# One hybrid decoder layer on one core: key low halves padded to 128 rows, sample and first prompt steps spaced otherwise, LayerNorm offset on another engine

## The chip, the cores and the metric

The kernel runs on one core of one Trainium2 chip. The core has a matrix engine (PE in the profile, with its weight loads shown apart as PEld), a vector engine (DVE), a scalar engine (ACT), a general engine (POOL, GpSimd) and an engine that here only issues transfers (SP, SyncE). Each engine works through its own list of instructions in a fixed order and waits on semaphores for the others. Sums of matrix products are collected in PSUM, a memory of eight banks; all else lies in SBUF or in the chip's main memory. The metric is the device time of one execution, in microseconds (us); smaller is better.

## What is computed

One layer for a prompt of 1024 positions and 8 samples of 4 new positions (32 rows), 1056 rows in all, model width 2048. The reference, cut to its core:

```python
z = rms_norm(x, norm_g) @ w_in                       # 2048 -> 7168
q, k, v, ga, u, vc, gb = split(z)                    # 7 x 1024
q, k = rope(q), rope(k)                              # 16 heads x 64
vc = layer_norm(gelu(vc), ln_g, ln_b); u = gelu(u)
o_attn = dilated_attention(q, k, v)                  # (128,1), (512,4), (2048,16), merged
o_chunk = u * (tril(w_s) @ vc + b_s)                 # chunks of 128 positions, 8 groups of 128
y = rms_norm(x + concat(o_attn * silu(ga), o_chunk * silu(gb)) @ w_out, final_g)
```

The samples attend to a cache of keys and values as well; of each sample 896 cached positions matter. Keys, values and the normalised `vc` are outputs too.

## The kernel before

**Products.** Every float32 operand of a product is split into a float16 high part and a float16 low part. A product is then three passes, high by high, high by low and low by high, summed in one PSUM bank. The projections (`proj_chunk`, line 181) take most of PE: 72 column tiles of 128 columns (56 of the input projection, 16 of the output projection), each 16 blocks of the contraction times 3 passes, over 1056 rows cut into 3 chunks of 352. One chunk is thus 48 matrix instructions of 128x352. There are three banks for the sums (`ps_p`), so a chunk can start only when the chunk three before it has been read.

**Fillers.** All other work is cut into steps, put in a queue by `set_steps` and called by `fill` after every 6 projection products. Each step has a cost that is only a place in the queue: steps are spread evenly by cost over the products of one or two column tiles. A step `wait(c)` does nothing and only takes up room. The instructions that a step issues are then ordered for each engine by a scheduler, so an engine can find the work of a later step ahead of that of an earlier one.

**Periods.** After eight column tiles for the gated channel input comes period 0, with the value, query and key tiles of the first head pair, and beside it the LayerNorm (`ln_steps`) of nine row tiles. For each: DVE adds the high and low part (L401), takes statistics (L414, L415), POOL takes a power (L245), DVE scales (L423, L424), POOL adds the offset `lb` (L428), ACT and DVE split the result again (L146, L147). In the same stretch DVE does the rotary step (`rope`, L468 to L475), which reads the two sums of query and key columns out of the banks, and the low parts of the weights (L139).

Then come eight periods, one for each head pair. A period has five or six column tiles. Beside the first ones run the prompt's attention (`prompt_steps`): 16 items, a query tile of 128 by a head, in slots that do the scores of one item (`fa`), the softmax of the one before (`fb`), the values of the one three before (`fc`) and the gate. A score is two instructions into one bank: L610 multiplies the query (high and low, 128 rows) by the key's high half (`khd`, the same 64 rows twice), and L611 multiplies the query's high 64 rows by the key's low half in `klo`, whose rows 0 to 63 belong to head 0 and rows 64 to 127 to head 1. The probabilities are turned by a transfer (L647) and multiplied by the values (L658, L665).

Beside the last two tiles of a period (`run_ab`, queries and keys of the next head pair) run the samples (`sample_steps`). For each of 8 samples `prep` splits the cached keys (hi on ACT L719, lo on DVE L722), loads two preparations further on (`load`, L711; two raw buffers `kvr`, three buffers each for `kvh` and `kvl`), and `s_mm` multiplies them (L750, L751). Then `soft1` turns the scores on PE (L770), takes minimum, exponential and quotient (L773, L785, L788), `soft2` turns the probabilities by a transfer (L798), and `pv_new` (L807) and `pv_mm` (L818, L819) multiply by the values, prepared in the same way with the hi part on POOL (L721).

The chunk mixing (`mix`) sums in a bank of `ps_t` (two banks, shared with the gate's and the samples' transposes), adds the bias into an SBUF tile `cf` (L901), multiplies by the gate (L902) and splits (L146, L147).

Of the kernel before, what the change touches and what calls it, by code (L numbers as in the profile page):

```python
# [8 lines left out]
F32 = mybir.dt.float32  # L9
# [45 lines left out]
def hybrid_step_kernel(  # L55
# [51 lines left out]

# [1 line left out]
    w_raw = {}  # L109
# [38 lines left out]

# [1 line left out]
    queue = []  # L150
# [37 lines left out]

# [1 line left out]
    def gelu2(ps, n, tp, *outs):  # L190
# [13 lines left out]

    # =============== start: normalised activations, first columns ===============
    tmp = pool("tmp")
# [141 lines left out]

    # =============== remaining columns of the gated channel input ===============
    SP.dma_start(out=lg, in_=ln_g.partition_broadcast(128))  # L350
# [18 lines left out]
    def spread(steps, at):  # L369
        # steps placed `at` steps apart  # L370
        out = []
        for c, f in steps:
            out += [(1e-3, lambda: None)] * at + [(c, f)]
        return out
# [17 lines left out]

    # =============== LayerNorm of the channel input ===============
    def ln_steps(i):
        t0, n = TILES[i]
        gt = {}

        def f0():
            if i < NQ:
                g = lnp.tile([128, 1024], F32, tag="gt", name="gt", bufs=3)  # L400
                DVE.tensor_tensor(out=g, in0=gnat[:, 0, i, :], in1=gnat[:, 1, i, :], op=ALU.add)  # L401
            else:
                vc_sample(0)
                vc_sample(4)
                g = gnat_s
            gt[0] = g

        def f1():
            f0()
            g = gt[0]  # L410
            bs = lnp.tile([128, 2, 6], F32, tag="bs", name="bs", bufs=2)
            mv = lnp.tile([128, 2], F32, tag="mv", name="mv", bufs=2)
            for hh in range(2):
                DVE.bn_stats(bs[0:n, hh, :], g[:, hh * 512:(hh + 1) * 512])  # L414
            DVE.bn_aggr(mv[0:n], bs[0:n])  # L415
            r = lnp.tile([128, 1], F32, tag="lr", name="lr", bufs=2)
            rsqrt(r[0:n], mv[0:n, 1:2], n, 1.0, lnp, "lm", EPS * VCS * VCS)
            st_[i] = (mv, r)

        def f2():  # L420
            mv, r = st_.pop(i)
            g = gt[0]
            DVE.tensor_scalar(g, g, mv[0:n, 0:1], r[0:n], ALU.subtract, ALU.mult)  # L423
            DVE.tensor_tensor(out=g, in0=g, in1=lg[0:n], op=ALU.mult)  # L424

        def f3():
            g = gt[0]
            POOL.tensor_tensor(out=g, in0=g, in1=lb[0:n], op=ALU.add)  # L428

        st_ = ln_state  # L430

        def f4():
            g = gt.pop(0)
            o = gnat[:, :, i, :] if i < NQ else lnp.tile([128, 2, 1024], F16, tag="gt", name="gt", bufs=3)
            hilo(g, o[0:n, 0, :], o[0:n, 1, :], VRS)
            SP.dma_start(out=vr_d[i, 0:n], in_=o[0:n])
            if i == NQ:
                SP.dma_start(out=vch, in_=g)

        return [(0.1, f1), (0.1, f2), (0.1, f3), (0.1, f4)]  # L440

    ln_state = {}

    # =============== per head pair / channel group ===============
    mid = pool("mid", left2)
# [7 lines left out]
    khd = [mid.tile([128, S], F16, name=f"khd{h}") for h in range(2)]  # L453
    klo = mid.tile([128, S], F16, name="klo")
    qbd = mid.tile([128, 2, DB, 2, DS], F16, name="qbd")
# [3 lines left out]
    gb = mid.tile([128, T], F32, name="gb")  # L459
    POOL.memset(qbd, 0.0)  # L460

    def rope(p, pa, pb, c0, n):
# [33 lines left out]
    def stack_load():  # L496
        for h in range(2):
            SP.dma_start(out=qst[h], in_=q_d[h].rearrange("l x r n -> (l x r) n"))
            kk = k_d[h].rearrange("l x r n -> l (x r) n")
            SP.dma_start(out=khd[h][0:64], in_=kk[0])  # L500
            SP.dma_start(out=khd[h][64:128], in_=kk[0])
            SP.dma_start(out=klo[64 * h:64 * h + 64], in_=kk[1])

# [33 lines left out]

    # period 0: first head pair, with the LayerNorm beside it
    MV, MA, MB, MG, MU, MGB = {}, {}, {}, {}, {}, {}
# [41 lines left out]

    # =============== attention and mixing pools ===============
    right = ExitStack()
# [9 lines left out]
    def prompt_steps(p):  # L593
        """per (query tile, head): scores, softmax, values; returns slots"""
        items = [(t, h) for t in range(NQ) for h in range(2)]
# [4 lines left out]
        def fa(i):  # L600
# [4 lines left out]
            tq = slice(t * 128, (t + 1) * 128)  # L605
            hi0 = 64 * h
            for j0 in range(0, nk, 512):
# [4 lines left out]
                    out=ps[:, 0:n],  # L612
                    lhsT=qst[h][hi0:hi0 + 64, tq],
                    rhs=klo[hi0:hi0 + 64, j0:j0 + n],
                    start=False,
# [70 lines left out]
        for s in range(n + 4):  # L686
            fs = []
            cost = 1.2
            if s - 4 >= 0 and (s - 4) % 2 == 1:
# [12 lines left out]
    def sample_steps(p, ahl):  # L702
# [139 lines left out]
        pre = [(0.05, lambda: load(0)), (0.05, lambda: load(1))]  # L842
        s1 = [(0.1, lambda: prep(0)), (0.2, s_new), (0.2, lambda: prep(1))]
        for b in range(DB):
            s1.append((0.4, lambda b=b: (s_mm(b), prep(b + 2))))
        s2 = [wait(0.8), (0.4, soft1), wait(1.0), (0.4, soft2), wait(0.6), (0.1, pv_new)]
        for b in range(DB):
# [30 lines left out]
    def mix(g, part, direct=False):  # L878
# [10 lines left out]
        else:  # L889
# [5 lines left out]
            bias = bb[:, 128:160]  # L895
        cf = ap_.tile([128, 512], F32, tag="cf", name="cf", bufs=1)
        if part < 2:
            o3, i3 = cf.rearrange("p (a b) -> p a b", a=4), pm.rearrange("p (a b) -> p a b", a=4)
        else:
            o3, i3 = cf[:, 0:n], pm[:, 0:n]  # L900
        DVE.scalar_tensor_tensor(out=o3, in0=i3, scalar=1.0 / (VRS * SWS), in1=bias, op0=ALU.mult, op1=ALU.add)  # L901
        DVE.tensor_tensor(out=cf[:, 0:n], in0=cf[:, 0:n], in1=gb[:, c0:c0 + n], op=ALU.mult)  # L902
# [105 lines left out]

    # =============== output projection ===============
    yt = {}  # L1010
# [76 lines left out]
    def sq(i, part):  # L1087
        """adds to the sum of squares, then scales by the final gain"""
        o, n = rows(i)
        c = slice(PARTS[part], PARTS[part + 1])  # L1090
        j = bank(ps_s, "s")
        ACT.activation(  # L1092
            out=j[0:n, 0:c.stop - c.start], in_=o[:, c], func=AF.Square, accum_out=ssq[0:n, i, part:part + 1]
        )
        DVE.tensor_tensor(out=o[:, c], in0=o[:, c], in1=fg[0:n, c], op=ALU.mult)  # L1095
# [21 lines left out]
    for j in range(1, NOUT - 2):  # L1117
# [9 lines left out]
        drain()  # L1127
    # the last two column tiles: rows are finished as their products end
    J = NOUT - 2
# [71 lines left out]
def _period(p):  # L1201
    """the column tiles of the input projection between two stages of the attention, in order"""
    if p == 0:
# [97 lines left out]
```

## Time and profile before

| | |
|---|---|
| time, median of 3 runs | 1927.72 us (1921.68 to 1928.16) |
| span of the profiled execution | 1919.8 us |
| busy: PE, DVE, ACT, POOL | 1839.0, 1081.7, 726.5, 142.4 us |
| projection products of 128x352 (three groups) | 9792 instructions |
| scores with the key's low half, L611 | 192 instructions, 64.1 us |

The span runs from the first to the last instruction of one profiled execution; the page prints no separate whole time for that execution, so what lies around the span is taken as the 7.9 us between it and the median. In the rows of a profile, `out<-in` names the tiles of the program, `xN` counts instructions, and a time in brackets is how long the engine stood idle before the instruction and what ended that. Matrix instructions overlap: their durations are longer than the distance from one start to the next, and it is this distance that counts.

### The profile page before, as it was taken

The page shows a single profiled execution, that of the slowest core. Times are in us where ns is not written, and L with a number is a line of the kernel's source. Part 1 is how long each engine was busy: PE and PEld are TensorE (multiplying, and loading weights), DVE is VectorE, ACT ScalarE, POOL GpSimd, SP SyncE. Part 2 cuts the span into 40 slices and gives each one's busy share as a digit, 9 for nine tenths or more (in the row PEclk, how much of TensorE's full clock was granted, in tenths as well). Part 3 has the DMA queues.
Part 4 walks back from the last instruction along what each step waited for, and adds up shares of the span by engine and source line. Part 5 has one row for each costly group of instructions (what it writes and reads, how often), then busy time and mean ns, then how long its engine had stood idle before and what let it go on. Part 6 is the DMA issues. An engine that isn't in the chain of part 4 may idle for free. (4 is left out here: it accounts for less than half of the span.)

```text
span 1919.8 us, 37195 instructions
## 1 busy us (share of the span) xinstructions
PE 1839.0 (96%) x15040; PEld 1222.4 (64%) x15040; DVE 1081.7 (56%) x2383; ACT 726.5 (38%) x1605; POOL 142.4 (7%) x146
## 2 busy tenths in 40 slices
PE   8999969999999999999999999999999999999997
PEld 7866645666566666666656666656666666666667
DVE  7633696646655665565556557557557543423344
ACT  7523214632542453254245236336336311212224
POOL 0000140001001000100100010010010020000001
PEclk9999989999999999999999999999999999999999
DMA  7423327566555646665565565566666598322324
GB/s 257 125 66 71 96 94 207 101 162 182 133 109 159 201 95 162 190 122 122 172 167 107 155 197 130 145 189 134 170 186 126 134 323 231 86 67 67 71 62 182
DMA packets 340415, 276.13 MB, mean 144 GB/s; under 512 B 255890, under 2 KB 291730, under 8 KB 338130
## 3 DMA queue, kind: packets, MB, share of 16 engines
q1 hardware_dynamic: 340242, 273.76, 54.8%
q8 instruction: 117, 1.92, 0.4%
q14 instruction: 56, 0.45, 0.1%
HBM read 179.85 MB, written 38.26 MB: 114 GB/s over the span
## 5 line engine op out<-in xcount | busy, mean ns | idle before, releaser
L181 PE MATMUL proj<-xh,wh 128*128 128x352 f16 (+3 forms) x3712 | 1113.7, 304 | 15.5 <-DVE ta L473 12.8
L181 PE MATMUL proj<-xh,wl 128*128 128x352 f16 (+3 forms) x3712 | 1112.1, 304 | 2.6 <-DVE wl L139 2.6
L181 PE MATMUL proj<-xl,wh 128*128 128x352 f16 (+3 forms) x3712 | 1112.3, 304 | 1.2 <-DVE xl L147 1.2
L181 PEld LDWEIGHTS <-wh 128*128 128x128 f16 x7424 | 692.0, 98 | 342.0 <-issue 27.1
L181 PEld LDWEIGHTS <-wl 128*128 128x128 f16 x3712 | 364.1, 98 | 176.9 <-DVE wl L139 3.2
L139 DVE SCALAR_TENSOR_TENSOR wl<-wraw,wh 128x512 f16<-128x512 f32 x288 | 198.1, 717 | 131.8 <-ACT wh L138 131.1
L138 ACT ACTIVATE wh<-wraw 128x512 f16<-128x512 f32 x288 | 166.0, 620 | 171.4 <-PE proj L181 163.8
L722 DVE SCALAR_TENSOR_TENSOR kvl<-kvr,kvh 128x896 f16<-128x896 f32 x128 | 141.7, 1107 | 133.7 <-ACT kvh L719 65.6
L631 ACT ACTIVATE sp<-sp,mn 128x256 f32<-128x256 f32 (+7 forms) x128 | 98.9, 772 | 133.1 <-DVE mn L619 133.1
L147 DVE SCALAR_TENSOR_TENSOR pn<-sp,pn 128x512 f16<-128x512 f32 (+2 forms) x192 | 106.1, 564 | 38.2 <-ACT pn L146 36.5
L721 POOL TENSOR_SCALAR kvh<-kvr 128x896 f16<-128x896 f32 x64 | 72.2, 1129 | 436.6 <-DMA kvr<-in_vc 197.1
L619 DVE CUSTOM_DVE_ANT_0 sp<-s,mp 128x512 f32<-128x512 f32 (+3 forms) x128 | 74.1, 584 | 50.9 <-PE s L611 49.7
L146 ACT ACTIVATE pn<-sp 128x512 f16<-128x512 f32 (+2 forms) x192 | 94.4, 515 | 7.5 <-DMA pt<-pn 4.9
L719 ACT ACTIVATE kvh<-kvr 128x896 f16<-128x896 f32 x64 | 60.6, 948 | 72.9 <-DMA kvr<-in_kc 60.4
L658 PE MATMUL o<-vst,pt 128*128 128x128 f16 x576 | 66.5, 220 | 9.0 <-DMA pt<-pn 9.0
L147 DVE SCALAR_TENSOR_TENSOR yhl<-proj,yhl 128x352 f16<-128x352 f32 (+1 forms) x42 | 21.4, 510 | 89.3 <-ACT yhl L146 89.3
L146 ACT ACTIVATE yhl<-proj 128x352 f16<-128x352 f32 (+1 forms) x42 | 18.8, 448 | 134.8 <-PE proj L181 115.4
L925 POOL TENSOR_TENSOR gb<-gb,tb 128x352 f32<-128x352 f32 x24 | 25.6, 1065 | 551.5 <-DVE tb L203 551.5
L638 DVE RECIPROCAL r<-den 128x1 f32<-128x1 f32 x128 | 20.8, 162 | 79.4 <-ACT sp L631 79.1
L611 PE MATMUL s<-klo,qst 64*128 64x512 f16 (+2 forms) x192 | 64.1, 334 | 0.3 <-DMA klo<-k_d 0.3
L610 PE MATMUL s<-khd,qst 128*128 128x512 f16 (+2 forms) x192 | 62.3, 331 | 1.5 <-DMA khd<-k_d 1.5
L665 PE MATMUL o<-vst,pt 128*128 128x64 f16 x576 | 62.9, 193 | 0.0
(166 smaller groups left out, 1569.5 us busy)
## 6 DMA issues: line engine op xcount, KB each, us to landing
wraw<-in_w_in SPq DMA_DIRECT2D x110, 512.0 KB, 5.0
kvr<-in_kc SPq DMA_DIRECT2D x64, 448.0 KB, 4.3
kvr<-in_vc SPq DMA_DIRECT2D x64, 448.0 KB, 3.8
wraw<-in_w_out SPq DMA_DIRECT2D x32, 512.0 KB, 5.1
yn<-in_x SPq DMA_DIRECT2D x8, 1024.0 KB, 8.7
out_y_p<-yn SPq DMA_DIRECT2D x16, 512.0 KB, 3.5
xn<-in_x SPq DMA_DIRECT2D x7, 1024.0 KB, 6.3
out_v_o<-tb SPq DMA_DIRECT2D x24, 176.0 KB, 2.5
```

Of the source, the lines that this page charges most:

```text
L138: ACT.activation(out=hi[:, sl, :], in_=r[:, rs, :], func=AF.Copy, scale=WS)
L139: DVE.scalar_tensor_tensor(out=lo[:, sl, :], in0=r[:, rs, :], scalar=WS, in1=hi[:, sl, :], op0=ALU.mult, op1=ALU.subtract)
L146: ACT.activation(out=hi, in_=src, func=AF.Copy, scale=scale)
L147: DVE.scalar_tensor_tensor(out=lo, in0=src, scalar=scale, in1=hi, op0=ALU.mult, op1=ALU.subtract)
L181: PE.matmul(out=ps[:, 0:n], lhsT=a[:, k, :], rhs=b[:, k, c0:c0 + n], start=(i == 0), stop=(i == 3 * KT - 1))
L611: PE.matmul(out=ps[:, 0:n], lhsT=qst[h][hi0:hi0 + 64, tq], rhs=klo[hi0:hi0 + 64, j0:j0 + n], start=False, stop=True,)
L619: DVE.tensor_tensor_reduce(sp[:, j0:j0 + n], ps[:, 0:n], mp[:, S - nk + j0:S - nk + j0 + n], 1.0 / (QS * KS), prev, ALU.add, ALU.min, mn,)
L631: ACT.activation(out=sp[:, 0:nk], in_=sp[:, 0:nk], func=AF.Exp, scale=-1.0, bias=prev, accum_out=den)
L658: PE.matmul(out=o[:, 0:128].rearrange("p (l c) -> p l c", l=2), lhsT=pt[:, j], rhs=vst[:, :, kb, h * HD:(h + 1) * HD], start=(kb == 0), st ...
L665: PE.matmul(out=o[:, 0:64], lhsT=pt[:, w + j], rhs=vst[:, 0, kb, h * HD:(h + 1) * HD], start=False, stop=(kb == nb - 1))
L721: POOL.tensor_scalar(hi, r, VS, 1.0, ALU.mult, ALU.mult)
L722: DVE.scalar_tensor_tensor(out=lo, in0=r, scalar=KS if j < DB else VS, in1=hi, op0=ALU.mult, op1=ALU.subtract)
```

## The change

Four things are changed.

1. The key's low half gets a tile for each head, `klo[0]` and `klo[1]`, of 128 rows, with the rows of the other head set to zero once. The second score instruction then takes all 128 rows of the query and of `klo[h]`.
2. The first five slots of a prompt block get the cost 2.0 instead of 1.2. In the samples' steps the second preparation comes ahead of `s_new`, a `wait(0.8)` stands ahead of the first `s_mm`, and the wait ahead of `pv_new` is 1.4 instead of 0.6.
3. The LayerNorm's offset is added by DVE instead of POOL.
4. The chunk mixing works in place in its PSUM bank; the tile `cf` is gone.

```diff
-            POOL.tensor_tensor(out=g, in0=g, in1=lb[0:n], op=ALU.add)
+            DVE.tensor_tensor(out=g, in0=g, in1=lb[0:n], op=ALU.add)
...
-    klo = mid.tile([128, S], F16, name="klo")
+    klo = [mid.tile([128, S], F16, name=f"klo{h}") for h in range(2)]
...
+    for h in range(2):
+        POOL.memset(klo[h][64 - 64 * h:128 - 64 * h], 0.0)
...
-            SP.dma_start(out=klo[64 * h:64 * h + 64], in_=kk[1])
+            SP.dma_start(out=klo[h][64 * h:64 * h + 64], in_=kk[1])
...
-            hi0 = 64 * h
...
-                    lhsT=qst[h][hi0:hi0 + 64, tq],
-                    rhs=klo[hi0:hi0 + 64, j0:j0 + n],
+                    lhsT=qst[h][:, tq],
+                    rhs=klo[h][:, j0:j0 + n],
...
-            cost = 1.2
+            cost = 1.2 if s > 4 else 2.0
...
-        s1 = [(0.1, lambda: prep(0)), (0.2, s_new), (0.2, lambda: prep(1))]
+        s1 = [(0.1, lambda: prep(0)), (0.1, lambda: prep(1)), (0.2, s_new), wait(0.8)]
...
-        s2 = [wait(0.8), (0.4, soft1), wait(1.0), (0.4, soft2), wait(0.6), (0.1, pv_new)]
+        s2 = [wait(0.8), (0.4, soft1), wait(1.0), (0.4, soft2), wait(1.4), (0.1, pv_new)]
...
-        cf = ap_.tile([128, 512], F32, tag="cf", name="cf", bufs=1)
-        if part < 2:
-            o3, i3 = cf.rearrange("p (a b) -> p a b", a=4), pm.rearrange("p (a b) -> p a b", a=4)
-        else:
-            o3, i3 = cf[:, 0:n], pm[:, 0:n]
-        DVE.scalar_tensor_tensor(out=o3, in0=i3, scalar=1.0 / (VRS * SWS), in1=bias, op0=ALU.mult, op1=ALU.add)
+        cf = pm
+        o3 = pm.rearrange("p (a b) -> p a b", a=4) if part < 2 else pm[:, 0:n]
+        DVE.scalar_tensor_tensor(out=o3, in0=o3, scalar=1.0 / (VRS * SWS), in1=bias, op0=ALU.mult, op1=ALU.add)
```

The lists of instructions show where this lands. First DVE in period 0, around the rotary step of the first chunk of 352 rows (`proj` are the sums of query and key columns, `gt` a LayerNorm tile, `gnat` its split result, `bs`, `mv` and `lm` its statistics). Before:

```order
L401 TENSOR_TENSOR gt<-gnat 128x1024
L415 BN_AGGR mv<-bs 128x2
L414 BN_STATS bs<-gt 128x6
L469 TENSOR_TENSOR tb<-proj,sin_t 128x352
L244 TENSOR_SCALAR lm<-mv 128x1
L147 SCALAR_TENSOR_TENSOR gnat<-gt,gnat 128x1024
L470 TENSOR_TENSOR o_3096<-ta,tb 128x352
L423 TENSOR_SCALAR gt<-gt,mv,lr 128x1024
L473 TENSOR_TENSOR ta<-proj,cos_t 128x352
L474 TENSOR_TENSOR tb<-proj,sin_t 128x352
```

And with the change (lines after the klo tiles are numbered two higher, so L471, L475 and L476 are the old L469, L473 and L474):

```order
L428 TENSOR_TENSOR gt<-gt,lb 128x1024
L244 TENSOR_SCALAR lm<-mv 128x1
L401 TENSOR_TENSOR gt<-gnat 128x1024
L423 TENSOR_SCALAR gt<-gt,mv,lr 128x1024
L414 BN_STATS bs<-gt 128x6
L424 TENSOR_TENSOR gt<-gt,lg 128x1024
L471 TENSOR_TENSOR tb<-proj,sin_t 128x352
L414 BN_STATS bs<-gt 128x6
L472 TENSOR_TENSOR o_3099<-ta,tb 128x352
L415 BN_AGGR mv<-bs 128x2
L147 SCALAR_TENSOR_TENSOR gnat<-gt,gnat 128x1024
L475 TENSOR_TENSOR ta<-proj,cos_t 128x352
```

The offset (L428) now stands on DVE; four of the nine come ahead of the last read of the first query sum (L474, now L476, the row behind the last one shown), and one L401, one L423, one L414 and one L147, which stood ahead of that read, stand behind it.

Second, DVE in the samples' softmax of the second period, from the ninth preparation on (`kvl` is a preparation's low part, `ss` the turned scores). Before:

```order
L722 SCALAR_TENSOR_TENSOR kvl<-kvr,kvh 128x896
L147 SCALAR_TENSOR_TENSOR qkhl<-o_7289,qkhl 128x704
L722 SCALAR_TENSOR_TENSOR kvl<-kvr,kvh 128x896
L773 ISA ss,mn<-t,msk 64x512
L773 ISA mn 64x1
L773 ISA ss,mn<-t,msk,mn 64x416
L773 ISA mn 64x1
L468 TENSOR_TENSOR ta<-proj,cos_t 128x352
L787 RECIPROCAL r<-den 64x1
```

And with the change:

```order
L723 SCALAR_TENSOR_TENSOR kvl<-kvr,kvh 128x896
L147 SCALAR_TENSOR_TENSOR qkhl<-o_7286,qkhl 128x704
L774 ISA ss,mn<-t,msk 64x512
L774 ISA mn 64x1
L723 SCALAR_TENSOR_TENSOR kvl<-kvr,kvh 128x896
L470 TENSOR_TENSOR ta<-proj,cos_t 128x352
L774 ISA ss,mn<-t,msk,mn 64x416
L774 ISA mn 64x1
L788 RECIPROCAL r<-den 64x1
```

The first half of the minimum moves ahead of the eleventh preparation's low part, and the second half moves behind the rotary step's first read (L470, the old L468). On PE, in the same period, 24 projection products instead of 18 stand between `s_new` and the first `s_mm`, 42 instead of 48 between the first and the sixth `s_mm`, 25 instead of 35 between the last `s_mm` and the turning of the scores (L770), and 72 instead of 60 between that and `pv_new`.

## The prediction

> **What bounds the kernel now.** I began with the page's busy times and the granted clock, then asked for PE's waits.
>
> ```profile
> span 1919.8 us, 37195 instructions
> PE 1839.0 (96%) x15040; PEld 1222.4 (64%) x15040; DVE 1081.7 (56%) x2383; ACT 726.5 (38%) x1605; POOL 142.4 (7%) x146
> core 0: 1919.8 us, clock 0.988
> ```
>
> PE is busy for 96% of the span, so PE sets the end and an edit pays only where it shortens PE's own work, one of its waits, or the time at a lower clock. The mean clock of 0.988 means that 0.012 x 1919.8 = 23 us were lost to a lower clock. The waits say where PE stood still:
>
> ```profile
> PE o L807 <- DMA pst<-pn: 12.9, 8, 2.3
> PE proj L181 <- DVE ta L473: 12.8, 2, 7.6
> PE s L750 <- ACT kvh L719: 10.0, 8, 2.7
> PE s L751 <- DVE kvl L722: 9.0, 11, 0.9
> PE o L658 <- DMA pt<-pn: 9.0, 10, 3.3
> ...
> PE proj L181 <- DVE wl L139: 2.6, 1, 2.6
> ...
> PE s L610 <- DMA khd<-k_d: 1.5, 3, 0.8
> ```
>
> The columns are total us, times and longest us. The samples cost 12.9 + 10.0 + 9.0 us, two places in the LayerNorm 12.8 + 2.6, the first prompt tiles 9.0 + 1.5. But a wait is not all that PE can lose, so I read the distances from start to start where the scores stand among other products:
>
> ```profile
> 498.53 0.19 PE L665 MATMUL o<-vst,pt 128*128 128x64 f16 x1
> ...
> 498.65 0.38 PE L610 MATMUL s<-khd,qst 128*128 128x512 f16 x1
> 498.96 0.39 PE L611 MATMUL s<-klo,qst 64*128 64x512 f16 x1
> 499.28 0.32 PE L181 MATMUL proj<-xh,wh 128*128 128x352 f16 x1
> 499.44 0.31 PE L181 MATMUL proj<-xl,wh 128*128 128x352 f16 x1
> 499.59 0.31 PE L181 MATMUL proj<-xh,wl 128*128 128x352 f16 x1
> ```
>
> A projection product of 352 columns takes 0.15 us from start to start. In proportion, 512 columns should take 0.15 x 512/352 = 0.218. L610 takes 0.31 until the 64-row L611 begins, and L611 takes 0.32 until the 128-row L181 begins: about 0.09 lost on entering the 64-row shape and 0.10 on leaving it. No wait names this loss.
>
> **The zero-padded low half.** There are 192 such instructions:
>
> ```profile
> L611 PE MATMUL s<-klo,qst 64*128 64x512 f16 (+2 forms) x192 | 64.1, 334 | 0.3 <-DMA klo<-k_d 0.3
> ```
>
> With 128 rows the second score has the shape of its neighbours. A product's length goes by its columns, which stay, so the padding itself costs nothing: L610 with 128 rows and L611 with 64 both show 0.38 to 0.39. The gain is 192 x (0.31 + 0.32 - 2 x 0.218) = 192 x 0.194 = **37 us**. Bounds: 0 if the gap belongs to the instruction and not to the shape, 37 if all of it goes. I take 37, since full-height neighbours such as L658 and L665 in the same list follow each other without a gap. The two memsets run once, at the opening of the pool, on an engine that is busy for 142 us in all and idle at that place; nothing on PE waits for them, and if something did, two instructions no longer than POOL's 2.34 us add (below) would cost 5 us once. The loads move the same bytes.
>
> The Trainium skill has a rule for this and one against it, on the page "TensorEngine Tiling (Array Packing)": under Key Properties, that a change of the tiling mode drains the engine, with which these rows agree at 0.09 to 0.10 us, and under Theoretical Speedup, that a contraction of at most 64 can go up to twice as fast in tiles of its own, which padding gives up. By the second this term would be no gain; it is weighed as a rival below.
>
> **The LayerNorm offset on DVE.** In the stretch from 214 to 300 us DVE is the bound:
>
> ```profile
> 214.00:300.00 86.00, 70.65 (x450) 45.01 (x448) 81.45 (x107) 21.28 (x32) 31.18 (x18) 0.94 0.39 116
> 256.03 2.34 POOL L428 TENSOR_TENSOR gt<-gt,lb 128x1024 f32<-128x1024 f32 x1 [2.72 <-DVE gt L424]
> 256.40 3.04 DVE L401 TENSOR_TENSOR gt<-gnat 128x1024 f32<-128x1024 f16 x1
> 263.54 0.45 PE L181 MATMUL proj<-xh,wh 128*128 128x352 f16 x1 [7.58 <-DVE ta L473]
> ```
>
> The first row has the busy times of PE, PEld, DVE, ACT and POOL and then the granted clock: DVE is busy for 81.45 of 86 us, at a clock of 0.94. The second and third row show why: while POOL adds an offset, a DVE instruction that normally takes 1.2 us takes 3.04. The groups of the window from 215 to 300 us, and the spread of L401, show its extent:
>
> ```profile
> L401 DVE TENSOR_TENSOR gt<-gnat x8: 1167/1996/3254, 217.7 to 273.4; 128x1024 f32<-128x1024 f16 x8
> L401 DVE TENSOR_TENSOR gt<-gnat 128x1024 f32<-128x1024 f16 x8 | 16.7, 2085 | 1.1 <-DMA gnat<-bighl 1.1
> L147 DVE SCALAR_TENSOR_TENSOR gnat<-gt,gnat 128x1024 f16<-128x1024 f32 x8 | 13.5, 1691 | 0.0
> L139 DVE SCALAR_TENSOR_TENSOR wl<-wraw,wh 128x512 f16<-128x512 f32 x11 | 11.0, 1029 | 0.0
> L424 DVE TENSOR_TENSOR gt<-gt,lg 128x1024 f32<-128x1024 f32 x8 | 9.7, 1212 | 0.0
> ...
> 296.52 0.67 DVE L139 SCALAR_TENSOR_TENSOR wl<-wraw,wh 128x512 f16<-128x512 f32 x1
> ```
>
> L401 loses 8 x (2085 - 1167) ns = 7.3 us; L147, taken at the 1.21 of L424 with as many elements, 8 x 0.48 = 3.8; L139, at 0.67 where POOL is idle (last row), 11 x 0.36 = 4.0: together 15.1, or 1.9 for each of the eight large POOL adds. The nine adds on DVE cost 9 x 1.21 = 10.9, the price of L424, which has the same shape. So DVE's work shrinks by only 4 us, but what counts is what stands ahead of PE. Up to the read that frees the first query sum, the new order has four adds more and four instructions less (one each of L401, L423, L414 and L147, 3.6 us together at their shortest); five collisions go. That is 4 x 1.2 - 3.6 - 5 x 1.9 = -8.3, so the read ends at about 255.2 instead of 263.5. PE arrives at 253.4 (263.54 - 7.58, less the 2.6 that it waited for L139, which had collided too) and waits 1.8. Carried on through the second chunk in the same way, nothing is added to it, so of 12.8 + 2.6 = 15.4 some 14 go: **14 us**. The clock lost 0.06 x 86 = 5.2 us here, right behind the long waits; I take 4.5 of it as gained. Bounds: if the long DVE instructions have another cause, 10.9 us of adds come on top and PE loses about 8; if all goes well, 15.4 + 5.2 = 20.6 are gained.
>
> **The samples' scores.** All but one of the long waits stand at the sixth sample:
>
> ```profile
> 745.25 9.14 SPq L711 DMA_DIRECT2D kvr<-in_kc x3
> ...
> 751.97 0.95 ACT L719 ACTIVATE kvh<-kvr 128x896 f16<-128x896 f32 x1 [2.91 <-DMA kvr<-in_kc]
> 752.97 0.18 PE L750 MATMUL s<-qbd,kvh 128*128 128x16 f16 x1 [1.25 <-ACT kvh L719]
> 754.10 0.18 PE L751 MATMUL s<-qbd,kvl 128*128 128x8 f16 x1 [0.94 <-DVE kvl L722]
> kvr<-in_kc SPq DMA_DIRECT2D x64, 448.0 KB, 4.3
> ```
>
> The load for it is issued at 745.25, when the fourth preparation has freed its buffer, and lands at 751.97, 6.7 us later, where the median is 4.3: weight loads and turned values are on the queue just ahead of it. PE waits about 1.4 us for the high part and 1.1 more for the low part. The change starts the scores 12 products (1.8 us) later, so the load comes out from behind that traffic and takes about 1.8 less, but packs the first six samples into 42 products instead of 48, so PE arrives 0.9 earlier. Net 0.9 less wait in seven periods: 6, less 1 for the denser last samples: **5 us** of 19.0. Bounds: -6 (the load is no faster: 7 x 0.9) to +15.
>
> **The samples' values.**
>
> ```profile
> 765.08 1.07 PE L770 MATMUL t<-eye_t,stsb 128*64 128x128 f32 x8
> 766.07 1.27 POOL L721 TENSOR_SCALAR kvh<-kvr 128x896 f16<-128x896 f32 x1 [2.14 <-DMA kvr<-in_vc]
> 768.38 0.68 DVE L773 CUSTOM_DVE_ANT_0 ss<-t,msk 64x512 f32<-64x512 f32 x1
> 777.09 0.23 PE L807 MATMUL o<-pst,vsn 32*128 32x128 f16 x1 [1.89 <-DMA pst<-pn]
> ```
>
> From the turning at 765.08 to the values at 777.09 PE has 60 products, the chain needs 12 us. The new order gives 72, 12 x 0.15 = 1.8 more. But the second half of the minimum still stands behind the eleventh preparation on DVE (waiting for POOL at 766.07, and that for its load), and since the turning now comes 10 products (1.5 us) sooner after the scores, that preparation is later against it: about 0.8 of the 1.8 is given back. 7 x 1.0 = 7; in the last period the values stand 13 products nearer, -1.9: **5 us** of 12.9. Bounds: -2 to 11.
>
> **First prompt tiles and mixing.** The first score now comes 14 products later in a period, so 1.5 us for `khd` goes; the first period's value product stands 12 products later, 1.8 of its 3.3 goes; in the others the value products have as many products ahead of them as before, but the drains that gave them time are gone, about 0.2 each: **2 us**. Bounds: -3 to 7. The mixing in place:
>
> ```profile
> L901 DVE SCALAR_TENSOR_TENSOR cf<-t,bb x24: 178/672/692, 387.7 to 1568.9; 128x512 f32<-128x512 f32 x16, 128x32 f32<-128x32 f32 x8
> L902 DVE TENSOR_TENSOR cf<-cf,gb x24: 182/684/693, 388.9 to 1569.1; 128x512 f32<-128x512 f32 x16, 128x32 f32<-128x32 f32 x8
> L146 ACT ACTIVATE chl<-cf x21: 229/622/631, 389.7 to 1514.8; 128x512 f16<-128x512 f32 x14, 128x32 f16<-128x32 f32 x7
> L147 DVE SCALAR_TENSOR_TENSOR chl<-cf,chl x21: 191/691/694, 390.4 to 1515.1; 128x512 f16<-128x512 f32 x14, 128x32 f16<-128x32 f32 x7
> ```
>
> L901 reads PSUM and L902 SBUF, at the same 0.67 to 0.68 us, so I cost the new operands at nothing. The bank is held for all four, 2.7 us (3.3 from first start to last end), instead of 0.7. Its next user is the second next transpose or mix, at least 24 products or 3.6 us behind: hidden.
>
> **Clock elsewhere.** Of the 23 us, 5.2 lie in the LayerNorm and some 3 at the idle end. Of the other 15, behind waits of 2 to 4 us in the samples and at the first tile, I take half: **7 us** (bounds 0 to 12).
>
> Sum: 37 + 14 + 4.5 + 5 + 5 + 2 + 7 = 74.5. The profiled span becomes 1845.3; with the 7.9 us around it, 1853, which is 1927.7 - 74.5.
>
> **Rivals.** (a) *The respacing gives nothing*: loads land as late as before and denser samples eat what the others gain; the last three small terms and most of the clock's 7 go: 74.5 - 18 = 56, 1871. For it: the two-buffer chain is unchanged. 12%. (b) *DVE in the LayerNorm gets worse*: the collisions are not POOL's. The term of 18.5 becomes -8, so 74.5 - 26.5 = 48, 1880. Against it: 3.04 starts 0.37 behind POOL's start and ends 1.07 behind its end. 5%. (c) *The padding does not do what it says*: the gap stays, 74.5 - 37 = 37, 1890. Against it: the gap stands on both sides of every L611 looked at, and a 128-row L610 or a projection stands between any two of them, so none could run beside another. 4%. The speed-up rule of the Trainium skill named above would give the same 1890, and the 0.32 us of L611, more than 0.218, speak against it. (d) *Slower*: the mixing's banks. If each of the 24 mixes made PE wait for the whole chain of 3.3 us, 24 x 3.3 = 79 us would be lost against 74.5 gained: 1932. It decides only if the two banks come round in less than 3.3 us instead of 3.6 or more, at every mix. 1.5%. (e) *More than forecast*: nearly all waits of the samples and the clock's losses go, 15 + 11 + 12 instead of 5 + 5 + 7: 1832. 5%.
>
> **How the numbers follow.** The forecast with its sizes a little off has 72.5%, and reaches from 1841 to 1866. The range takes in (a) and (b) and part of (e): 1838 to 1883. Faster by over 0.5% (about what a measurement of this kernel can tell from no change): all but (d) and a sliver, 97.5%; within 0.5% 1%; slower 1.5%.
>
> **What would show it.** Right: L612 with 128 rows, starts 0.22 apart on both sides of it; no DVE instruction of 3 us between 214 and 300 and PE's wait there under 3 us; clock above 0.992; the wait ahead of `pv_new` halved; POOL without L428. Wrong: distances of 0.31 around the second score, a wait of PE on a `t` bank, or waits on `kvh` and `kvl` above 19 us.

## The result, and the profile after

| | before | changed |
|---|---|---|
| time, median (4 runs each) | 1927.37 us (1921.68 to 1928.16) | 1883.76 us (1881.56 to 1887.17) |
| span of the profiled execution | 1919.8 us | 1879.8 us |

The ratio is 0.9775, with a 95% interval from 0.9756 to 0.9794: 44 us faster, where 74.5 were forecast. 1883.76 lies 0.8 us above the upper end of the range. One step of the sum fell at once: the profiled run of the changed kernel took 1881.56 us, 1.8 above its span, and the runs of before stand as close to theirs, so the 7.9 us "around the span" were mostly the distance of a fast profiled run from the median. The two spans, 40.0 us apart, are to be held against the 74.5.

The page and PE's waits after, in the same columns as before (total us, times, longest us):

```profile
span 1879.8 us, 37188 instructions
PE 1790.0 (95%) x15040; PEld 1220.3 (65%) x15040; DVE 1085.5 (58%) x2392; ACT 724.5 (39%) x1605; POOL 125.2 (7%) x139
core 0: 1879.8 us, clock 0.995
PE o L659 <- DMA pt<-pn: 17.4, 12, 4.9
PE o L819 <- POOL kvh L722: 9.4, 7, 2.4
PE o L808 <- DMA pst<-pn: 9.4, 8, 2.1
PE s L751 <- ACT kvh L720: 7.9, 10, 1.8
PE o L820 <- DVE kvl L723: 7.0, 10, 1.6
PE s L752 <- DVE kvl L723: 6.0, 7, 0.9
PE t L677 <- DVE onat L671: 4.7, 3, 1.7
PE proj L181 <- DVE ta L475: 2.9, 1, 2.9
```

And three rows of before that the prediction did not use:

```profile
PE o L818 <- POOL kvh L721: 2.6, 6, 0.9
PE o L819 <- DVE kvl L722: 0.8, 1, 0.8
PE t L676 <- DVE onat L670: 0.3, 1, 0.3
```

The two waits that the change was forecast to shorten most did shorten: the LayerNorm's from 15.4 to 3.3 us (2.9 above and 0.4 for `wl`), the samples' scores from 19.0 to 13.9. But the sum of all of PE's waits in this view rose, from 71.8 to 81.1 us. First prompt tiles (L659) went from 9.0 to 17.4, the values of V from 3.4 to 16.4, the gate's transposes from 0.3 to 4.7.

The gaps at the second score are gone. A place in the changed kernel, start to start:

```profile
486.43 0.38 PE L611 MATMUL s<-khd,qst 128*128 128x512 f16 x1
486.64 0.38 PE L612 MATMUL s<-klo,qst 128*128 128x512 f16 x1
486.86 0.31 PE L181 MATMUL proj<-xh,wh 128*128 128x352 f16 x1
```

Both distances are 0.21 to 0.22 us, where they were 0.31 and 0.32. Over all 192 pairs the median loss was 97 ns on entering and 103 ns on leaving the 64-row shape; now both are 0. That is 192 x 0.200 = 38.4 us that PE certainly no longer spends there.

In the LayerNorm, the group of L401 between 214 and 300 us and the same stretch as one window (busy us of PE, PEld, DVE, ACT, POOL, then the granted clock):

```profile
L401 DVE TENSOR_TENSOR gt<-gnat 128x1024 f32<-128x1024 f16 x8 | 9.7, 1208 | 1.5 <-DMA gnat<-bighl 1.5
214.00:300.00 86.00, 83.06 (x550) 54.16 (x549) 80.08 (x128) 22.67 (x35) 10.87 (x9) 0.98 0.45 132
```

L401 takes 1208 ns instead of 2085: without POOL's adds no DVE instruction takes 3 us, and PE is busy for 83.1 of 86 us instead of 70.7, at a clock of 0.98 instead of 0.94. So both mechanisms worked as forecast. The samples' loads did as well: from issue to landing the sixth tile of keys takes 4.5 us instead of 6.5 (mean of the first seven periods), where 1.8 less was forecast. The question for the runs is where their gain went.

### The profile page after: what moved, and what is told of

Its sections match the earlier page's. It is cut to its first block, busy times and chain, and to the rows that moved or that the text cites. A ratio compares the mean times of both kernels' runs of the same rounds, so it can differ in the third digit from the quotient of the medians.

```text
span 1879.8 us, 37188 instructions
## 1 busy us (share of the span) xinstructions
PE 1790.0 (95%) x15040; PEld 1220.3 (65%) x15040; DVE 1085.5 (58%) x2392; ACT 724.5 (39%) x1605; POOL 125.2 (7%) x139
## 5 line engine op out<-in xcount | busy, mean ns | idle before, releaser
L139 DVE SCALAR_TENSOR_TENSOR wl<-wraw,wh 128x512 f16<-128x512 f32 x288 | 202.3, 730 | 124.8 <-ACT wh L138 123.9
L147 DVE SCALAR_TENSOR_TENSOR pn<-sp,pn 128x512 f16<-128x512 f32 (+2 forms) x192 | 106.4, 565 | 33.5 <-ACT pn L146 32.7
L659 PE MATMUL o<-vst,pt 128*128 128x128 f16 x576 | 66.5, 220 | 21.0 <-DMA pt<-pn 17.4
L147 DVE SCALAR_TENSOR_TENSOR yhl<-proj,yhl 128x352 f16<-128x352 f32 (+1 forms) x42 | 21.4, 510 | 92.3 <-ACT yhl L146 92.3
L659 PEld LDWEIGHTS <-pt 128*128 128x128 f16 x576 | 52.1, 98 | 28.5 <-DMA pt<-pn 18.5
L639 DVE RECIPROCAL r<-den 128x1 f32<-128x1 f32 x128 | 20.8, 162 | 81.1 <-ACT sp L632 80.9
L611 PE MATMUL s<-khd,qst 128*128 128x512 f16 (+2 forms) x192 | 61.7, 327 | 0.9 <-DVE mn L620 0.9
```

Of the source, the lines that this page charges most:

```text
L139: DVE.scalar_tensor_tensor(out=lo[:, sl, :], in0=r[:, rs, :], scalar=WS, in1=hi[:, sl, :], op0=ALU.mult, op1=ALU.subtract)
L147: DVE.scalar_tensor_tensor(out=lo, in0=src, scalar=scale, in1=hi, op0=ALU.mult, op1=ALU.subtract)
L611: PE.matmul(out=ps[:, 0:n], lhsT=qst[h][:, tq], rhs=khd[h][:, j0:j0 + n], start=True, stop=False)
L659: PE.matmul(out=o[:, 0:128].rearrange("p (l c) -> p l c", l=2), lhsT=pt[:, j], rhs=vst[:, :, kb, h * HD:(h + 1) * HD], start=(kb == 0), st ...
```

## The experiments

Every run was timed against the kernel before on the same chip; the difference given is between the two medians, with the ratio's interval.

### Each part by itself

**The LayerNorm's offset alone**, on the kernel before:

```diff
-            POOL.tensor_tensor(out=g, in0=g, in1=lb[0:n], op=ALU.add)
+            DVE.tensor_tensor(out=g, in0=g, in1=lb[0:n], op=ALU.add)
```

> The kernel before with the LayerNorm's offset on VectorE alone. Theory (the 3-us VectorE instructions are collisions with GpSimd's adds): the waits of 15.4 us there go but for 1 to 3, and the clock there is higher, 12 to 17 us faster, 1911 to 1916; if the end of the LayerNorm moves later against PE, the first prompt tile of period 1 takes back up to 7, 1921. Rival (the long instructions have another cause): 9 adds x 1.21 us come on top, 8 us slower, 1935.

Measured: 1919.48 us, 8.7 faster, ratio 0.9952 (0.9936 to 0.9967). The waits in the trace:

```profile
PE s L750 <- ACT kvh L719: 13.4, 9, 3.2
PE o L658 <- DMA pt<-pn: 12.8, 10, 5.5
...
PE proj L181 <- DVE ta L473: 4.1, 2, 3.2
```

The LayerNorm's wait fell by about 11 us, as the theory said, and the rival is out. The gain is less than the theory's 12 to 17 us and lies in its second case, in which the first prompt tile takes some back. Of the 14 us by which the first prompt score starts earlier, 4 are lost again before the first sample score: the first value product now waits 5.5 us instead of 3.3, and a stretch at half clock follows it. Over the whole run the first prompt tiles took back 3.8 us and the samples' high parts 3.4, the samples' new values gave 3.3, and all waits together fell by 5.4 us (71.8 to 66.4).

**The padding alone**, with the mixing in its bank, which makes room for it (the two edits of the key's low half and of `cf` in the diff above; without the second, 58.8 KB per partition are left for a pool that needs 60.5):

> The kernel before with the padded low key halves and the mixing in its bank alone (the padding needs the 2 KB per partition that the mixing's copy gives up). Theory of the cover (the gaps of 38 us go, but they gave time to chains whose length does not change: turned probabilities of first prompt tiles, gate transposes, sample loads; PE waits there instead): gaps 0, those waits 12 us longer in sum than before, 24 to 28 us faster, 1900 to 1904. Rival (the gaps are a clean gain; the shortfall comes from the LayerNorm): 36 to 38 us faster, 1890.

Measured: 1905.39 us, 24.7 faster, ratio 0.9869 (0.9851 to 0.9886), inside the theory's 24 to 28 and far from 38. **The mixing alone**, to take its share out:

> The kernel before with the mixing in its bank alone, to take it out of the run with the padding. Theory (the four steps hold the bank for 3 us, but its next user is further off): within 2 us of before. Rival (gate transposes and mixes wait for the bank): up to 24 x 1.1 = 26 us slower.

Measured: 1933.42 us, 3.3 slower, ratio 1.001 (0.9996 to 1.0023), no difference clear of noise and at most 4.4 us; one wait of 1.1 us for the bank is in its trace. So the padding itself is worth about 25 us of its 38, some 3 more if the mixing's 3.3 are real. The waits with the padding:

```profile
PE o L808 <- DMA pst<-pn: 13.1, 8, 2.7
...
PE o L659 <- DMA pt<-pn: 12.7, 11, 3.7
PE s L751 <- ACT kvh L720: 12.1, 9, 3.2
...
PE o L819 <- POOL kvh L722: 4.9, 5, 1.3
PE t L677 <- DVE onat L671: 4.4, 3, 1.8
...
PE s L611 <- DMA khd<-k_d: 3.1, 7, 0.8
```

No row is large, and nearly every one grew: first prompt tiles by 3.7, gate transposes by 4.1, the samples' high parts by 2.1, V's by 2.3, the keys by 1.6. All waits of this view sum to 93.1 us against 71.8, so by the two traces 21 of the 38 us that no longer pass between scores pass in waits, where 12 were expected. That is one execution of each kernel, and their spans differ by only 14.6 us; by the medians 38.4 - 24.7 = 13.7 us come back. So it is 14 to 21 us, a third to a little over half.

**The three spacings alone**, on the kernel before:

```diff
-            cost = 1.2
+            cost = 1.2 if s > 4 else 2.0
...
-        s1 = [(0.1, lambda: prep(0)), (0.2, s_new), (0.2, lambda: prep(1))]
+        s1 = [(0.1, lambda: prep(0)), (0.1, lambda: prep(1)), (0.2, s_new), wait(0.8)]
...
-        s2 = [wait(0.8), (0.4, soft1), wait(1.0), (0.4, soft2), wait(0.6), (0.1, pv_new)]
+        s2 = [wait(0.8), (0.4, soft1), wait(1.0), (0.4, soft2), wait(1.4), (0.1, pv_new)]
```

> The kernel before with the three spacings alone (cost of the first prompt tiles' steps, samples' preparations, wait ahead of the samples' new values). Theory (the spacing gains 5 in the samples' scores and 3.5 at the new values, and loses 13 at the samples' values V and some 5 at first prompt tiles and gate transposes, since the low part of a late preparation now stands behind weight splits on VectorE): 2 to 12 us slower, 1930 to 1940. Rival (the losses come with PE being faster through padding and LayerNorm, and the spacing itself gains what was predicted): 10 to 12 us faster, 1916.

and **the changed kernel without them**:

> The changed kernel with the three spacings taken back (padding, LayerNorm and mixing in place stay). Theory (the spacing causes the waits at V and at first prompt tiles): waits at V fall from 16 to about 4 us, those ahead of first prompt tiles' values from 21 to about 12, the samples' scores and new values lose 8 again: 1868 to 1880, faster than the changed kernel. Rival (a faster PE meets these waits in any case): V still waits 10 us or more, and with the gain of 8.5 in scores and new values gone the time is 1890 or more.

Measured: alone 1912.28 us, 15.9 faster, ratio 0.9915 (0.9899 to 0.9932); without them 1892.8 us, 9.0 slower than the changed kernel. The theory with which I began, that the spacing causes the loss, fell in both runs, and the gain alone is larger than the rival's 10 to 12. The half of it about V is right. V's rows with the spacing alone:

```profile
PE o L818 <- POOL kvh L721: 8.1, 8, 2.2
...
PE o L819 <- DVE kvl L722: 6.3, 9, 1.5
```

V waits 14.4 us there, and 3.2 in the changed kernel without the spacing. But the spacing pays for that elsewhere, above all in the clock: besides the one at the idle end there are 5 stretches at half clock where before has 9, and in the changed kernel 3 where it has 11 without the spacing. The other timed executions say the same: the mean granted clock is 0.992 to 0.995 with the spacing alone against 0.985 to 0.990 in the 13 executions of before beside it, and 0.991 to 0.995 in the changed kernel against 0.987 to 0.991 without the spacing. By the means of these clocks that is an estimated 12 of the 15.9 us and 7 of the 9.0.

### Which of the spacings, and what stands at the two new waits

**Prompt cost back**, and **the samples' two spacings back**, each in the changed kernel:

> The changed kernel with the first prompt tiles' cost back at 1.2, the samples' spacing kept. Theory (at first prompt tiles the wait is that of a chain of fixed length; the cost only shifts it between scores, values and gate transposes): within 3 us of 1884. Prediction's term: 2 us slower. Rival (the raised cost crowds the later tiles and makes the gate transposes wait, 4.4 us): 4 to 8 us faster.

> The changed kernel with the samples' two spacings taken back, the prompt cost kept. Theory (they put 8 products, 1.2 us, into a stretch of fixed length in seven periods, and part waits that halve the clock): 8 us for the products and 4 to 10 for the clock slower, 1896 to 1902 less what V no longer waits; at least 1892. Rival (the samples' spacing only moves waits from scores and new values to V): within 3 us of 1884.

Measured: 1881.55 us without the prompt cost, 2 us from the changed kernel and within the scatter; 1895.6 us without the samples' spacing, 12 slower, as the theory said. The prompt cost is worth nothing, and the samples' spacing is the whole of it.

**Period 1's loads later.** In the changed kernel the first prompt tile of period 1 waits longest. SP's issues and PE's wait there:

```profile
305.66 5.80 SPq L858 DMA_DIRECT2D vr<-vr_d  x8
...
313.33 1.22 SPq L648 DMA_TRANSPOSE pt<-pn  x1
...
316.56 0.27 PE L659 MATMUL o<-vst,pt 128*128 128x128 f16 x1 [4.89 <-DMA pt<-pn]
```

Eight loads of 0.7 us each stand ahead of the first transfer that turns probabilities. In the run they are asked for later:

```diff
-            mix_load(g)
+            if g > 0:
+                mix_load(g)
...
+            if g == 0:
+                mix_load(g)
             run_m(MV[p], merge(a4, mix_steps(g)), v_evac(p))
```

> The changed kernel with period 1's loads for the mixing issued later, so that only 3 instead of 11 small loads stand on SP ahead of the first turned prompt probabilities. Theory (that burst causes the wait of 4.9 us at 311 and part of the next three, and the two half-clock slices behind them): 5 to 9 us faster, 1875 to 1879. Rival (the late LayerNorm memory sets the first prompt tile, whatever stands on SP): 0 to 2 us.

Measured: 1884.89 us, no gain, as the rival said, though what it named as the cause is not shown by this run. The first transfer went out at 307.24 instead of 313.33, and the wait behind it fell from 4.9 to 3.2 us, but two others of the same period grew:

```profile
315.14 0.26 PE L659 MATMUL o<-vst,pt 128*128 128x128 f16 x1 [3.17 <-DMA pt<-pn]
326.72 0.22 PE L659 MATMUL o<-vst,pt 128*128 128x128 f16 x1 [3.23 <-ACT ta L195]
332.50 0.47 PE L677 MATMUL t<-eye_t,onat 128*128 128x128 f32 x1 [2.81 <-DVE onat L671]
```

**V's preparations one group earlier.** With the spacing, the low half of the sixth cached V tile stands on DVE behind a rotary read and four weight splits. The run puts it ahead of them again and leaves everything else where it was:

```diff
-        s2 = [..., (0.4, soft2), wait(1.4), (0.1, pv_new)]
+        s2 = [..., (0.4, soft2), wait(0.7), (0.1, lambda: prep(DB + 2)), wait(0.6), (0.1, pv_new)]
...
-            s2.append((0.4, lambda b=b: (pv_mm(b), prep(DB + b + 2) if b < DB - 2 else None)))
+            s2.append((0.4, lambda b=b: (pv_mm(b), prep(DB + b + 3) if b < DB - 3 else None)))
```

> The changed kernel with each preparation of V one group of value products earlier (the fourth buffer use is the same, the place of the first new-value product too), which puts the sixth low half on VectorE ahead of the rope's read and the four weight splits, where it stood in before. Theory (the order on VectorE causes the waits of 16.4 us at V): they fall to 3 to 7, 9 to 13 us faster, 1871 to 1875. Rival (the loads of V set them, two buffers deep): V still waits over 12 us and the time is within 3 us of 1884.

Measured: 1883.21 us. V still waits 12.3 us, and the time is that of the changed kernel: the rival holds here too. The order on DVE made only 4 of the 16 us.

### A third buffer for the samples' loads

Two experiments had moved a wait and won nothing. So I measured the whole stretch of the samples, from the first product with cached keys to the last with cached values. In the period that begins near 740 us, before and changed:

```profile
742.64 0.17 PE L750 MATMUL s<-qbd,kvh 128*128 128x16 f16 x1
...
795.05 0.17 PE L819 MATMUL o<-pst,kvl 128*128 128x8 f16 x1
```

```profile
723.12 0.17 PE L751 MATMUL s<-qbd,kvh 128*128 128x16 f16 x1
...
774.91 0.17 PE L820 MATMUL o<-pst,kvl 128*128 128x8 f16 x1
```

That is 52.4 and 51.8 us. The mean of the first seven periods is 52.7 before, 52.9 with the spacings alone, 53.8 with the padding alone, 53.1 changed and 53.0 with V's preparations earlier, although the spacing puts 269 projection products into the stretch instead of 261. A length that does not follow PE's work is set by something else; the candidate is the pair of load buffers. The run takes every third tile into a buffer of the prompt's scores, which the samples use only once:

```diff
-            t = ap_.tile([128, NKEY], F32, tag="kvr", name="kvr", bufs=2)
+            if j % 3 == 2:
+                t = ap_.tile([128, S], F32, tag="sp", name="kvs", bufs=2)[:, 0:NKEY]
+            else:
+                t = ap_.tile([128, NKEY], F32, tag="kvr", name="kvr", bufs=2)
...
-            load(j + 2)
+            load(j + 3)
...
-        s1 = [(0.1, lambda: prep(0)), ...
+        s1 = [(0.05, lambda: load(2)), (0.1, lambda: prep(0)), ...
```

> The changed kernel with a third buffer for the samples' loads (every third cached tile is loaded into one of the two buffers of the prompt's scores, which the samples use once; loads are issued three tiles ahead instead of two). Theory (from the first cached score to the last cached value a period takes 53 us in every kernel so far, whatever the spacing and whatever PE does in it, because two load buffers set it): that stretch falls to 46 to 50, the waits at scores and V from 30 to under 15, 1845 to 1865. Rival (the DMA engines, or VectorE's low halves, set it): the stretch stays over 52, within 5 us of 1884.

Measured: the stretch falls to 45.1 us, below even the theory's 46 to 50, with 240 products in it; and the time is 1885.13 us, unchanged, as the rival said. Neither was right alone. The same period and the waits show why:

```profile
724.45 0.17 PE L754 MATMUL s<-qbd,kvh 128*128 128x16 f16 x1
...
769.69 0.17 PE L823 MATMUL o<-pst,kvl 128*128 128x8 f16 x1
```

```profile
PE t L677 <- DVE onat L671: 17.9, 8, 3.3
PE o L659 <- DMA pt<-pn: 14.6, 12, 5.9
PE o L823 <- DVE kvl L726: 9.5, 9, 1.4
...
PE s L611 <- DMA khd<-k_d: 5.8, 7, 1.5
```

29 products, 4.3 us, left the stretch, so it is 3.7 us shorter by itself, and waits at scores and V fall from 30.3 to 11.3. That much speaks for the load buffers. But the last gate transpose of each period now waits 2.2 us on average, 17.9 in all instead of 4.7, and the stacked keys 5.8.

**The same without the three spacings:**

> The third buffer in the kernel without the three spacings. Theory (the spacing pays only because it puts 8 more products into a stretch that the loads hold at 53 us, and parts the waits so that the clock is not halved; with the loads out of the way neither matters): within 5 us of the third buffer with the spacings. Rival (the spacing has a worth of its own): 8 to 12 us slower than that.

Measured: 1899.99 us, 14.9 slower than with them: a miss. The samples' new values wait 17.2 us there instead of 7.2, the stacked keys 12.2 instead of 5.8, and 21 us are lost to half clock instead of 11. The spacing has a worth that does not hang on the loads.

**The gate and the first scores parted further**, with and without the third buffer:

```diff
+            if s == n + 3:
+                slots.append(wait(0.8))
             slots.append((cost, lambda fs=fs: [f() for f in fs]))
...
-        return [wait(1.5)] + pr
+        return [wait(2.1)] + pr
```

> The third buffer, and two more products' spacings: a step of 0.8 ahead of the last gate transpose of a period and 2.1 instead of 1.5 ahead of its first score. Theory (the third buffer did shorten the samples' stretch from 53 to 45 us with 4 us less work in it; what PE saved there it waited at the last gate transpose, 17.9 instead of 4.7 us, and for the stacked keys, 8.8 instead of 0.3): with both parted further these fall to under 8 and under 4, and 10 to 20 us stay, 1865 to 1875. Rival (the chain from scores to gate has a fixed length whatever its spacing, so the wait moves on to the turned probabilities): waits there rise by as much, within 4 us of 1885.

> The changed kernel with the same two spacings, without the third buffer. Theory: gate waits of 4.7 us go, nothing else does, since the loads still hold the samples' stretch: 1878 to 1883. Rival (the two spacings are what was missing, not the buffer): as fast as the run with both.

Measured: with the buffer **1871.32 us** (1867.33 to 1874.59), ratio 0.970 (0.9677 to 0.9723); without it 1885.32 us, ratio 0.9776 (0.976 to 0.9791). That is the theory's 1865 to 1875; without the buffer it is 2 us over the 1878 to 1883 that was expected, and the second rival is out. Neither edit does anything by itself and together they win 12 to 14 us: this version beats both kernels. Its waits:

```profile
PE o L659 <- DMA pt<-pn: 10.6, 12, 2.0
...
PE s L611 <- DMA khd<-k_d: 7.9, 7, 2.3
...
PE o L659 <- DVE onat L671: 6.2, 10, 1.4
PE o L659 <- ACT pn L146: 4.7, 2, 4.5
...
PE t L677 <- DVE onat L671: 2.9, 4, 1.1
```

The gate's wait went from 17.9 to 2.9 us. Part of it came back, as the first rival said: the values' waits for `onat` and `pn` rose from 3.4 to 10.9 us, those for `pt` fell from 14.6 to 10.6, and all waits together fell from 78.4 to 68.2. The keys' wait did not fall (7.9, where under 4 was expected), so the later first score seems to add nothing; it wasn't run apart.

**The padding taken out of that version**, to see whether it is worth its 38 us where the other chains are shorter:

> The version with the third buffer and the two spacings, but with the 64-row low score of before (the padding alone taken out). Theory (the padding was worth 25 instead of 38 us only because PE ran into chains of fixed length; where these are shortened and parted it is worth more): 30 to 38 us slower than with the padding, 1901 to 1909. Rival (the padding is worth 25 us in any surroundings, something in it costs the rest): 1894 to 1898.

Measured: 1889.19 us, 17.9 slower than with the padding: less than either side expected. The waits without it:

```profile
PE o L657 <- DMA pt<-pn: 8.4, 7, 3.3
...
PE o L657 <- DVE onat L669: 4.2, 4, 2.0
...
PE t L675 <- DVE onat L669: 0.8, 1, 0.8
```

All waits sum to 50.8 us here and to 68.2 with the padding. So the padding returns 17 us as waits in this version, and by the medians 38.4 - 17.9 = 20.5 us; on the kernel before it was 21 by the traces and 14 by the medians. The return is about half in this version and a third to a half on the kernel before, so parting two of the chains did not lower it as the theory expected. By the rows of the two versions, most of it comes at the prompt's own products: values waiting for `pt`, `onat` and `pn`, and gates, 13.4 us without the padding and 24.4 with it.

## Why the prediction was wrong

Term by term, from the two traces:

| step | forecast | in the traces |
|---|---|---|
| padding, gaps of L611 | 37 | 38.4 |
| LayerNorm, PE's waits | 14 | 12.1 (15.4 to 3.3) |
| clock, both terms | 11.5 | 12.4 (half-clock stretches cost 23.1, now 10.7) |
| samples' scores | 5 | 5.1 (19.0 to 13.9) |
| samples' new values | 5 | 3.5 (12.9 to 9.4) |
| first prompt tiles, keys, gates | 2 | -15 (11 to 26) |
| V's values | no term | -13.0 (3.4 to 16.4) |
| mixing | 0 | 0 |

The right column sums to 43, against 40.0 between the spans, so some 3 us are in no row. The runs give a second account: alone, the LayerNorm's edit is worth 8.7 us of its 18.5, the padding 24.7 of 37 and the spacings 15.9 of 19 (5 + 5 + 2 and the clock's 7), 49.3 in sum and 43.6 together. The mechanisms of the padding, the LayerNorm and the samples' loads are in the traces, near their sizes; what did not hold is that their gains stay.

What failed is the step "in the others the value products have as many products ahead of them as before, but the drains that gave them time are gone, about 0.2 each: 2 us" with its bounds of -3 to 7. I counted what the padding takes from PE and not what the same 38 us did for others. A prompt item's softmax, transfer and split take their time on DVE, ACT and the queue whatever PE does, and its value product stands a fixed number of products behind. Each gap of 0.2 us in between was time for that chain, and by the order of the slots (scores in slot i, values in slot i+3) the scores of two more items lie between, with two to four such gaps, not one.

The same step let 1.8 of the first value product's 3.3 us go; with the LayerNorm's edit PE comes there earlier, and the waits of the first tiles of period 1 grow from 3.3 to 7.2 us with that edit alone and to 8.7 in the changed kernel. The runs show which edit did it: the rows of first prompt tiles, keys and gates (11.1 us before) grow by 12.8 us with the padding alone and by 4.5 with the LayerNorm's edit alone, and shrink by 3.3 with the spacings alone. The whole return of the padding is 14 us on the kernel before by the medians and 21 by the traces, 20 and 17 in the best version.

The second miss is the absent term for V. The prediction weighed the samples' loads at the scores and at the new values and stopped there; V takes its tiles from the same two buffers. V's wait grows by 11.0 us with the spacings alone, by 2.9 with the padding alone and by 2.5 with the LayerNorm's edit alone. The stretch is 53 to 54 us long in every kernel with two buffers, so what the spacing saved at its head came back at its end. Rival (a) had the reason ("the two-buffer chain is unchanged") but not the result: the spacing is worth 9 to 16 us nevertheless, because parted waits keep the clock up, and, as far as can be worked out, because 8 more products fit into a stretch of fixed length (7 x 8 x 0.15 = 8 us). The second cannot be the whole of the rest, since the spacing is worth 14.9 us with the third buffer too. The LayerNorm's term was right to the first prompt score, 14 us earlier; what was late next was the first tile of period 1, and in the time of that part alone 8.7 of 18.5 us are left.

Of the signs to look for, the score's distances, DVE's durations and POOL's rows came out as written, the clock nearly so (0.995 in the profiled execution, 0.991 and 0.992 in the others, where above 0.992 was named); the wait ahead of `pv_new` fell by a quarter, not by half; and the waits on `kvh` and `kvl` rose from 22.4 to 30.3 us, the sign named for a wrong prediction (its bound of 19 counted the scores alone, which fell to 13.9; the growth is V's). Rivals (b), (c) and (d) are out: no long DVE instruction, no gap, no wait for a mix bank beyond 1.1 us. That (b) and (c) would have given 1880 and 1890 is chance.

What stays open: which chain sets the first tiles of period 1 once the loads are out of the way (its waits sum to 8.7 us in the changed kernel and 9.8 with the third buffer), why the keys' wait did not fall with a later first score, and how much of the padding comes back exactly, since the traces and the medians differ by 3 to 8 us.

## What to carry to other kernels

When an edit takes time from the engine that sets the end, list the chains that ran beside that time, count how many of the removed pieces lay inside each, and take the sum as what may come back as waits; here a third to a half did. Before parting or reordering steps, measure whether a stretch's length follows the engine's work at all: one that kept its 53 us under five variants was held, at least in part, by its buffers, and a wait removed inside it came back at its end. A longer chain can hide behind another, so an edit that wins nothing (the third buffer, the two later steps) may still be half of one that does.

## What the runs showed of the hardware

Waits cost more than their length when two of them fall together. The changed kernel without the spacings, in slices of 3.41 us (busy us of PE, PEld, DVE, ACT, POOL, then the granted clock):

```profile
729.27:732.69 3.42, 3.42 (x48) 2.46 (x46) 0.56 (x2) 0.36 (x1) 0.00 (x0) 1.00 0.92 325
732.69:736.10 3.41, 1.28 (x20) 0.73 (x18) 1.68 (x2) 1.90 (x2) 0.00 (x0) 0.99 0.35 136
736.10:739.51 3.41, 3.41 (x27) 1.94 (x25) 0.50 (x1) 0.69 (x1) 0.00 (x0) 0.51 0.81 234
```

In the second slice PE waited 1.19 us for a high part and 0.94 for a low part; in the third it ran at half clock, 27 products instead of 48, a loss of 1.7 us. The changed kernel has the same pair of waits at 410 us, 1.21 and 0.94, across the border of two slices:

```profile
406.46:409.87 3.41, 2.39 (x28) 1.46 (x26) 0.15 (x1) 0.82 (x1) 0.00 (x0) 1.00 0.62 248
409.87:413.29 3.42, 2.29 (x26) 1.61 (x27) 2.19 (x2) 1.08 (x2) 0.00 (x0) 1.00 0.28 67
413.29:416.70 3.41, 1.88 (x25) 1.13 (x22) 0.53 (x1) 0.77 (x1) 0.00 (x0) 1.00 0.58 207
```

The clock stays up. All half-clock stretches of a run lie on one grid of 3.41 us. Over the 16 traces of this case, without the first and last 20 us of each and with PE's share of a slice taken from its products' starts and columns, a slice at full clock with a share under 0.36 was followed by half clock 104 times in 104, one from 0.36 to 0.40 9 times in 30, and one above 0.40 never, in 8403. So waits of some 2.1 us in one slice cost 1.7 us more, and the same waits parted cost nothing more; that is where much of the samples' spacing has its worth. The Trainium skill, "TensorE: Matmul & The Clock Gate" (Part 1), gives the same window, 3413 ns and free-running, but lets the clock fall after an idle window of about 3.4 us; here a slice in which PE still streamed a third of the time was enough.
